# A decoder layer in fp32r pieces: four gate pairs moved ahead of attention as seven products each, branch tiles moved into attention

## The chip, the cores and the metric

The kernel runs on one core of one Trainium2 chip. Its metric is the device time of one execution in microseconds. The kernel before takes 628.67 us, the median of three runs (628.64, 628.67 and 631.46). The profiled execution took 629.03 us, of which the profile's span covers 627.3.

## The reference

The kernel computes one post-norm decoder layer on x of 512 tokens by 1024 channels, all in float32. Cut to what matters here:

```python
proj = h @ w_in                                  # 1024 -> q 512 | k 512 | v 512 | p 512 | g 2048
y_attn = moba_attention(q, k, v, rel_bias) @ w_branch_attn      # 8 heads x 64, causal, T5 bias
y_pool = multiscale_pool(p, w_pool_group, pool_scale) @ w_branch_pool
gates = sigmoid(g)                               # two gates of 1024 channels
mixed = gates[:, :, 0] * y_attn + gates[:, :, 1] * y_pool
h = layer_norm(ALPHA * h + mixed @ w_out)
a, u = split(h @ w_ffn_in)                       # 2 x 2816
f = (gelu(causal_dwconv(a)) * u) @ w_ffn_out
out = layer_norm(ALPHA * h + f)
```

With 512 tokens and blocks of 256 each token attends causally to all earlier tokens.

## The kernel before, in words

**Precision.** Every large product is made of three fp32r matmuls: each operand is split into a high part (a rounding copy, on ScalarE) and a low part (the rest, a subtraction on VectorE), and `mm3` (L247) issues hi x hi, lo x hi and hi x lo. A weight chunk of 128x1024 comes by DMA into one of three raw buffers (`wraw`, `araw`), `split` (L73) makes `whi` on ScalarE and `wlo` on VectorE, and five such slots form a ring. `weights` (L241) has up to three chunks fetched ahead of the one in use.

**Tiles.** Activations are kept transposed: channels on partitions, 512 tokens on the free axis. The tile (f) of a gate or branch is 128 output channels by 512 tokens in one PSUM bank; there are eight banks. An ordinary tile of the input projection (`in_tile`, L488) is 8 contraction steps x 3 matmuls of 512 columns.

**Seven products.** `seven` (L293) makes two tiles at once from two weight chunks by a Strassen-like scheme: weights and x are cut into 2x2 blocks, sums of blocks are formed, and seven products replace eight. One product is 4 steps x 3 matmuls of 256 columns. For each pair it needs the chunks A (1024 wide), X (1024), D (512) and Y (1024); X is loaded with one plain DMA on SP's queue and a second, accumulating one on GpSimd's (POOL) queue (`fetch_raw`, L182). Y is formed on VectorE from X and A. The sums of x (`T3`, `nT1`, `nT2`, `T4`, each as hi and lo, 512 KB apiece) are the same for all pairs.

**Stages, in the order in which TensorE meets them.** The v projection; two ordinary pooling tiles; five pairs by seven products (pool 0 and 1, then q and k in four pairs), with the pooling mixer's vector work beside them; attention for eight heads; seven branch tiles (`br`, f 0 to 6, pooling half and attention half); four gate pairs (f 4 to 7) by seven products, with sums of x formed anew from x loaded again (`quad`); the last branch tile; the output projection with LayerNorm; the FFN.

**Attention.** For head h, `head(h)` makes scaled and split q and k (L441 to L452, with a DMA for each half), `scores(h)` (L533) multiplies them, adds the bias strip and takes the row maximum (L553, VectorE), exponentials with row sums (L559, ScalarE), reciprocals (L561, VectorE) and the normalisation (L564, POOL, four instructions); `trans(h)` transposes the result (L619) and copies it to `PT` with one copy on ScalarE (L621) and two on VectorE; `pv(p)` multiplies `PT` of two heads with `vv` (L632). Each step of the loop over heads also holds one ordinary gate tile (`g0`, `g8`, `g1`, ...), whose raw logits are copied to `gates` (L498); these eight tiles are f 0 to 3 of both gates.

**Order.** The program is traced in this order and a scheduler reorders it within each engine by its own cost model, so an engine's instructions stand in one fixed sequence, and each engine works its sequence strictly in order. `tc.issue_after` holds an instruction back behind another in that sequence. Tiles with one tag share buffers in turn: three bias strips, three `pp`, three raw buffers, two `PT`; a tile that takes over memory waits for the last reader of what lay there.

## Time and profile before

| | |
|---|---|
| three runs | 628.64, 628.67, 631.46 us |
| profiled execution | 629.03 us, span 627.3 us |
| TensorE (PE) busy | 617.3 us (98%) |
| VectorE (DVE) busy | 505.0 us (81%) |
| ScalarE (ACT) busy | 354.0 us (56%) |
| GpSimd (POOL) busy | 118.5 us (19%) |
| DMA | 107.70 MB, mean 172 GB/s |

In the profile PE is the TensorE matmul, PEld its weight load, and SPq and POOLq the queues from which SyncE and GpSimd issue DMAs. A matmul's listed duration overlaps the next one's, so the pace of TensorE is read from one start to the next. The same holds, by less than 0.1 us, for VectorE and ScalarE.

### The profile page before, as it was taken

The page shows a single profiled execution, that of the slowest core. Times are in us where ns is not written, and L with a number is a line of the kernel's source. Part 1 is how long each engine was busy: PE and PEld are TensorE (multiplying, and loading weights), DVE is VectorE, ACT ScalarE, POOL GpSimd, SP SyncE. Part 2 cuts the span into 40 slices and gives each one's busy share as a digit, 9 for nine tenths or more (in the row PEclk, how much of TensorE's full clock was granted, in tenths as well). Part 3 has the DMA queues.
Part 4 walks back from the last instruction along what each step waited for, and adds up shares of the span by engine and source line. Part 5 has one row for each costly group of instructions (what it writes and reads, how often), then busy time and mean ns, then how long its engine had stood idle before and what let it go on. Part 6 is the DMA issues. An engine that isn't in the chain of part 4 may idle for free.

```text
span 627.3 us, 10417 instructions
## 1 busy us (share of the span) xinstructions
PE 617.3 (98%) x3988; PEld 553.3 (88%) x3988; DVE 505.0 (81%) x780; ACT 354.0 (56%) x536; POOL 118.5 (19%) x131
## 2 busy tenths in 40 slices
PE   9999999999999999999999999999999999999994
PEld 6899998777788998889999999999999888888884
DVE  6978787776494788399998988898988769698796
ACT  6636777655634567115576566566656346555452
POOL 0133134323142101110110101011000302123302
PEclk9999999999999999999999999999999999999998
DMA  8467647522547515704568687688734995899905
GB/s 325 152 193 191 171 120 225 134 76 84 168 116 216 139 60 177 304 32 152 151 161 200 195 200 181 178 195 203 190 100 150 331 256 117 208 212 211 261 1 134
DMA packets 40545, 107.70 MB, mean 172 GB/s; under 512 B 4384, under 2 KB 4648, under 8 KB 40240
## 3 DMA queue, kind: packets, MB, share of 16 engines
q1 hardware_dynamic: 27264, 71.90, 34.2%
q0 software_dynamic: 12656, 34.10, 27.9%
q10 hardware_dynamic: 576, 1.05, 0.5%
q8 instruction: 31, 0.51, 0.3%
q14 instruction: 18, 0.15, 0.1%
HBM read 101.77 MB, written 3.17 MB: 167 GB/s over the span
## 4 chain that ended last, share of the span: by engine, by line
PE 98%; DVE 1%; DMA 1%; ACT 0%; DVEq 0%; issue 0%
PE saf L252 5%; PE saf L249 5%; PE saf L253 5%; PE fi L249 3%; PE fi L252 3%; PE v L426 3%; PE fi L253 3%; PE sbf L252 3%; PE sbf L253 2%; PE sbf L249 2%; PE br L249 2%; PE g L249 2%; PE g L253 2%; PE g L252 2%; PE br L252 2%; PE wo L252 2%
## 5 line engine op out<-in xcount | busy, mean ns | idle before, releaser
L77 ACT ACTIVATE whi<-wraw 128x1024 fp32r<-128x1024 f32 (+1 forms) x53 | 53.9, 1024 | 44.3 <-DMA wraw<-in_w_fo 8.5
L78 DVE TENSOR_TENSOR wlo<-wraw,whi 128x1024 fp32r<-128x1024 f32 (+1 forms) x53 | 65.2, 1237 | 14.3 <-ACT whi L77 14.0
L78 DVE TENSOR_TENSOR wlo<-araw,whi 128x1024 fp32r<-128x1024 f32 x52 | 63.2, 1224 | 10.2 <-ACT whi L77 9.8
L77 ACT ACTIVATE whi<-araw 128x1024 fp32r<-128x1024 f32 x52 | 54.4, 1057 | 18.1 <-PE saf L252 5.3
L199 POOL DMA_DIRECT2D xraw<-in_w_fi x15 | 18.0, 1203 | 136.4 <-DMA xraw<-in_w_fi 45.5
L77 ACT ACTIVATE whi<-tw 128x1024 fp32r<-128x1024 f32 (+1 forms) x30 | 29.4, 983 | 24.4 <-DMA tw<-in_w_fo 11.3
L78 DVE TENSOR_TENSOR wlo<-tw,whi 128x1024 fp32r<-128x1024 f32 (+1 forms) x30 | 33.3, 1126 | 8.0 <-ACT whi L77 8.0
L252 PE MATMUL sbf<-T_lo,whi 128*128 128x256 f32 x136 | 37.9, 279 | 0.0
L252 PE MATMUL saf<-nT_lo,whi 128*128 128x256 f32 x136 | 37.8, 278 | 0.0
L249 PE MATMUL saf<-nT_hi,whi 128*128 128x256 f32 x136 | 37.8, 278 | 0.0
L252 PE MATMUL saf<-hT_lo,whi 128*128 128x256 f32 x136 | 37.8, 278 | 0.0
L249 PE MATMUL saf<-hT_hi,whi 128*128 128x256 f32 x136 | 37.8, 278 | 0.0
L253 PE MATMUL saf<-hT_hi,wlo 128*128 128x256 f32 x136 | 37.7, 278 | 0.0
L249 PE MATMUL sbf<-T_hi,whi 128*128 128x256 f32 x136 | 37.7, 277 | 0.0
L253 PE MATMUL sbf<-T_hi,wlo 128*128 128x256 f32 x136 | 37.7, 277 | 0.0
L253 PE MATMUL saf<-nT_hi,wlo 128*128 128x256 f32 x136 | 37.7, 277 | 0.0
L249 PE MATMUL fi<-hT_hi,whi 128*128 128x256 f32 (+1 forms) x112 | 36.2, 328 | 0.2 <-ACT hT_hi L77 0.2
L252 PE MATMUL fi<-hT_lo,whi 128*128 128x256 f32 (+1 forms) x112 | 36.5, 327 | 0.0
L253 PE MATMUL fi<-hT_hi,wlo 128*128 128x256 f32 (+1 forms) x112 | 36.3, 326 | 0.0
L564 POOL TENSOR_SCALAR pp<-pp,rs 128x128 f32<-128x128 f32 (+3 forms) x32 | 25.2, 801 | 36.7 <-DVE rs L561 26.6
L237 POOL DMA_DIRECT2D tw<-in_w_fo x18 | 15.6, 897 | 60.7 <-DVE wlo L78 60.7
L559 ACT ACTIVATE pp<-pp,nm 128x128 f32<-128x128 f32 (+3 forms) x32 | 17.6, 552 | 15.3 <-DVE nm L556 15.2
(346 smaller groups left out, 2172.8 us busy)
## 6 DMA issues: line engine op xcount, KB each, us to landing
tw<-in_w_fo POOLq DMA_DIRECT2D x20, 512.0 KB, 8.5
araw<-in_w_fi SPq DMA_DIRECT2D x17, 512.0 KB, 3.6
xraw<-in_w_fi SPq DMA_DIRECT2D x15, 512.0 KB, 4.7
xraw<-in_w_fi POOLq DMA_DIRECT2D x15, 512.0 KB, 6.1
wraw<-in_w_c SPq DMA_DIRECT2D x10, 512.0 KB, 3.9
wraw<-in_w_fi SPq DMA_DIRECT2D x10, 512.0 KB, 4.2
wraw<-in_w_fo SPq DMA_DIRECT2D x10, 512.0 KB, 7.4
tw<-in_w_fo SPq DMA_DIRECT2D x10, 512.0 KB, 7.8
```

Source lines behind the costliest of these rows:

```text
L77: state["hi"] = nc.scalar.activation(hi, src, AF.Copy)
L78: state["lo"] = nc.vector.tensor_tensor(lo, src, hi.bitcast(F32), op=ALU.subtract)
L199: state["acc"] = nc.gpsimd.dma_start(v, bass.AP(tensor=a.tensor, offset=a.offset, ap=[[pst, pn], [u.offset + S - a.offset, 2], [est, S]]), ...
L237: nc.gpsimd.dma_start(raw, half(then[1:], sl), accum_op=ALU.add)
L249: ins = nc.tensor.matmul(out_, wh, ah, start=start, stop=False, **kw)
L252: nc.tensor.matmul(out_, wh, al, start=False, stop=False, **kw)
L253: nc.tensor.matmul(out_, wl, ah, start=False, stop=stop, **kw)
L426: nc.tensor.matmul(bs[j], xs_[j][a], (wh, wl)[b], start=kt == 0 and n == 0, stop=False)
L559: exps[h] = nc.scalar.activation(pp[:, offs[i]:offs[i] + n], pp[:, offs[i]:offs[i] + n], AF.Exp, bias=nm[:, i:i + 1], accum_out=rs[:, i:i ...
L564: nc.gpsimd.tensor_scalar(pp[:, offs[i]:offs[i] + n], pp[:, offs[i]:offs[i] + n], rs[:, i:i + 1], 1.0, op0=ALU.mult, op1=ALU.mult)
```

## The change

Gate tiles f 0 to 3 are no longer ordinary tiles inside attention. They become four pairs by seven products, run straight after the q/k pairs, with the same sums of x, which are still in memory then. Their logits are written straight to `gates`, copied and put through the sigmoid there.

In attention the place of the gate tiles is taken by the pooling halves of branch tiles f 0 to 6 (12 matmuls of 512 columns each, against 24 of a gate tile), so z is split before the loop over heads. Heads run further ahead: scores of heads 0, 1 and 2 stand among the pairs, and inside the loop `scores(h + 3)` follows step h. After attention the attention halves follow, `br6` first. The branch weights are packed anew so that a chunk holds two halves.

To make room, v is written to DRAM (`v_d`) and read back (`vv`) when the pairs are through, and the eight sums of x are written to DRAM (`form_d`) during the pairs and read back after attention, which replaces loading x again and forming the sums a second time. The copy of the attention output to `oT` and its later split become one split from PSUM.

```diff
+    add_gates(range(GSEVEN))
+    halves = [(f, 1) for f in range(KT - 1)] + [(f, 0) for f in BR0]
...
+    aside = [(n, q) for n in ("T3", "nT2", "T4", "nT1") for q in range(2)]
+    def put_aside(count):
+        with tc.issue_after(state["plain"].ins):
+            for n, q in aside[:count]:
+                nc.sync.dma_start(form_d[n, q], flat(ti[n][q]))
+        del aside[:count]
...
+    put_aside(1)
+    head(2, nms[0], exps[0])
+    scores(1)
+    for f in range(GSEVEN):
+        n = 1 + pairs + f
+        gslot[f], gslot[8 + f] = gates[:, f, :], gates[:, GSEVEN + f, :]
+        seven(("g", f), (xT_hi, xT_lo), ti, xr[1][:, 2, n % 2 * 256:n % 2 * 256 + 256], gslot[8 + f],
+              lambda ba, u, f=f: gate_raw(f, ba))
+        if f == 0:
+            put_aside(2)
+            scores(2)
+        elif f == 1:
+            head(3, nms[1], exps[1])
+    with tc.issue_after(exps[2].ins):
+        flush()
+        for f in range(GSEVEN):
+            nc.scalar.activation(gslot[f], gslot[f], AF.Sigmoid)
+            state["gate"] = nc.scalar.activation(gslot[8 + f], gslot[8 + f], AF.Sigmoid, scale=-1.0)
...
+    vv = ap.tile([P, NT, H * DH], F32, name="vv", bufs=1)
+    nc.gpsimd.dma_start(vv, v_d)
...
-        state["o"] = nc.scalar.activation(oT[:, p, :], b, AF.Copy)
+        split(oT_hi[:, p, :], oT_lo[:, p, :], b)
...
+    for k in range(4):
+        split(zT_hi[:, k, :], zT_lo[:, k, :], zT[:, k, :])
     for h in range(H):
-        if h + 2 < H:
-            head(h + 2, nms[h], exps[h])
-        if h < H - 1:
-            in_tile(*fill.pop(0))
-        if h + 2 < H:
-            scores(h + 2)
+        if h + 4 < H:
+            head(h + 4, nms[h + 2], exps[h + 2])
         with ExitStack() as held:
             if h and h % 2 == 0:
                 pv(h // 2 - 1)
                 held.enter_context(tc.issue_after(state["pv"].ins))
             trans(h)
-        if h >= 4:
-            with tc.issue_after(nms[h].ins), tc.issue_after(exps[h].ins):
-                split(zT_hi[:, h - 4, :], zT_lo[:, h - 4, :], zT[:, h - 4, :])
-        if h == H - 1:
-            in_tile(*fill.pop(0))
+        if h:
+            br_tile(h - 1, 1)
+        if h + 3 < H:
+            with tc.issue_after(state["gate"].ins):
+                scores(h + 3)
...
-        nc.gpsimd.dma_start(quads[n], xT[k.start * P:k.stop * P, t].rearrange("(k p) t -> p k t", p=P))
+    for n in ("T3", "nT2", "T4", "nT1"):
+        for q in range(2):
+            nc.gpsimd.dma_start(flat(tg[n][q]), form_d[n, q])
...
-            t_form(forms[0], tg, *quads)
```

**VectorE at the start of attention.** Before, the first `PT` copies stand between the maxima of head 2 (`nm`, from the PSUM tile `sc2`) and those of head 3:

```order
L553 ISA pp2_1185,nm2_1186<-sc2_3_1190,strip2_937 128x512
L553 ISA nm2_1186 128x1
L622 COPY PT0_1213<-tr0_1_1215 128x512
L623 COPY PT0_1213<-tr0_2_1216 128x256
L78 TENSOR_TENSOR wlo31_1329<-wraw31_1327,whi31_1328 128x1024
```

Now, with the maxima of head 3 just done, two heads' copies and the split of z stand together:

```order
L572 ISA pp3_1722,nm3_1723<-sc3_3_1727,strip3_1116 128x512
L572 ISA nm3_1723 128x1
L79 TENSOR_TENSOR wlo45_1778<-wraw45_1776,whi45_1777 128x1024
L316 TENSOR_TENSOR sag3_1534<-xr1_99,scg3_1535 128x256
L575 TENSOR_SCALAR nm3_1723<-nm3_1723 128x4
L688 COPY PT0_1703<-tr0_1_1705 128x512
L689 COPY PT0_1703<-tr0_2_1706 128x256
L688 COPY PT1_1759<-tr1_1_1761 128x512
L689 COPY PT1_1759<-tr1_2_1762 128x256
L79 TENSOR_TENSOR zT_lo_1679<-zT_78,zT_hi_1678 128x512 x3
L572 ISA pp4_1798,nm4_1799<-sc4_01_1801,strip4_1266 128x128
```

The low parts of z, which the first branch tile multiplies, have moved from the loop's second half to a place behind four copies.

**ScalarE at the same place, now.** `whi` and `zT_hi` are high parts, `gates<-sag3` is the raw copy of the last pair's logits:

```order
L578 ACT_TABLE_LOAD
L578 ACTIVATE pp3_1722,rs3_1724<-pp3_1722,nm3_1723 128x128
L578 ACTIVATE pp3_1722,rs3_1724<-pp3_1722,nm3_1723 128x256
L578 ACTIVATE pp3_1722,rs3_1724<-pp3_1722,nm3_1723 128x384
L578 ACTIVATE pp3_1722,rs3_1724<-pp3_1722,nm3_1723 128x512
L466 ACTIVATE k1_5_1751<-rk2_817 64x512
L469 ACTIVATE q1_5_1750<-rq2_1034 64x4x128
L627 ACTIVATE gates_79<-sag3_1534 128x512
L687 ACTIVATE PT1_1759<-tr1_0_1760 128x512
L78 ACTIVATE whi46_1934<-wraw46_1933 128x1024
L645 ACT_TABLE_LOAD
L645 ACTIVATE gates_79<-gates_79 128x512
```

Right ahead of these rows stand the four `zT_hi` and the `PT0` copy. The copy of head 1 stands behind the exponentials of head 3, and two table loads have come in.

**POOL at the same place, now.** `strip6` is the bias strip of head 6, `pp3` the normalisation of head 3:

```order
L399 DMA strip6_1796<-F_d_179 128x512
L653 DMA vv_1684<-v_d_180 128x2048
L399 DMA strip7_1877<-F_d_179 128x512
L583 TENSOR_SCALAR pp3_1722<-pp3_1722,rs3_1724 128x128
```

Before, `vv` lay in memory from the start; now its load is queued behind `strip6`, which waits for the maxima of head 3.

## Rows read from the trace of the kernel before

**Rows 1.** The page: span, busy time of each engine, the chain by engine.

```profile
span 627.3 us, 10417 instructions
...
PE 617.3 (98%) x3988; PEld 553.3 (88%) x3988; DVE 505.0 (81%) x780; ACT 354.0 (56%) x536; POOL 118.5 (19%) x131
...
PE 98%; DVE 1%; DMA 1%; ACT 0%; DVEq 0%; issue 0%
```

**Rows 2.** Waits of PE: line, waited for, us in total, times, longest.

```profile
PE warm_ps L341 <- DVE warm L338: 1.2, 1, 1.2
PE fi L249 <- ACT hT_hi L77: 0.2, 1, 0.2
```

**Rows 3.** Windows: length, engines' busy us, clock, DMA share, GB/s.

```profile
66.00:72.00 6.00, 6.00 (x47) 5.39 (x46) 3.51 (x7) 3.31 (x5) 0.15 (x1) 1.00 0.94 241
98.00:163.00 65.00, 65.00 (x368) 51.65 (x366) 45.44 (x106) 36.49 (x81) 20.78 (x29) 1.00 0.38 108
...
201.00:246.00 45.00, 45.00 (x365) 43.92 (x364) 34.49 (x44) 26.86 (x41) 5.07 (x4) 1.00 0.47 133
```

**Rows 4.** Timeline of PE: start, us, instruction; 512 columns, then 256.

```profile
138.05 0.39 PE L249 MATMUL g<-xT_hi,whi 128*128 128x512 f32 x1
...
142.14 0.39 PE L249 MATMUL g<-xT_hi,whi 128*128 128x512 f32 x1
```

**Rows 5.** The same, of a late gate pair.

```profile
227.74 0.28 PE L249 MATMUL sag<-xT_hi,whi 128*128 128x256 f32 x1
...
229.94 0.28 PE L252 MATMUL sag<-gnT_lo,whi 128*128 128x256 f32 x1
```

**Rows 6.** Timeline of DVE in attention.

```profile
144.66 1.22 DVE L78 TENSOR_TENSOR wlo<-wraw,whi 128x1024 fp32r<-128x1024 f32 x1
145.80 0.68 DVE L553 CUSTOM_DVE_ANT_0 pp<-sc,strip 128x512 f32<-128x512 f32 x1
...
146.41 0.68 DVE L622 COPY PT<-tr 128x512 f32<-128x512 f32 x1
147.01 0.41 DVE L623 COPY PT<-tr 128x256 f32<-128x256 f32 x1
147.34 0.16 DVE L556 TENSOR_SCALAR nm<-nm 128x4 f32<-128x4 f32 x1
```

**Rows 7.** Timeline of ACT in attention.

```profile
130.58 0.40 ACT L559 ACTIVATE pp<-pp,nm 128x128 f32<-128x128 f32 x1 [3.33 <-DVE nm L556]
...
132.90 0.63 ACT L445 ACTIVATE k<-rk 64x512 fp32r<-64x512 f32 x1
...
134.07 0.63 ACT L77 ACTIVATE zT_hi<-zT 128x512 fp32r<-128x512 f32 x1
134.61 1.04 ACT L77 ACTIVATE whi<-wraw 128x1024 fp32r<-128x1024 f32 x1
```

**Rows 8.** Timeline of ACT: the table load ahead of the first exponential.

```profile
81.34 1.28 ACT L559 ACT_TABLE_LOAD   x1 [0.48 <-DVE nm L556]
82.64 0.40 ACT L559 ACTIVATE pp<-pp,nm 128x128 f32<-128x128 f32 x1
```

**Rows 9.** DMA issues: tiles, queue, count, KB each, median us to landing.

```profile
quad<-in_xT POOLq DMA_DIRECT2D x4, 512.0 KB, 5.9
...
quad<-in_w_c POOLq DMA_DIRECT2D x4, 512.0 KB, 8.5
...
lnb<-in_lnr POOLq DMA_DIRECT2D x2, 1024.0 KB, 11.1
```

**Rows 10.** Timeline of POOL: loads of x (quad), xs and lnb.

```profile
163.83 3.04 POOL L675 DMA_DIRECT2D quad<-in_xT  x4 [10.12 <-PE ob L632]
...
255.66 2.19 POOL L757 DMA_DIRECT2D xs<-in_x  x4 [6.67 <-DVE mx_lo L78]
...
270.66 2.79 POOL L762 TENSOR_SCALAR lnb<-lnb 128x1024 f32<-128x1024 f32 x1 [12.28 <-DMA lnb<-in_lnr]
```

**Rows 11.** DMA from 154 to 206 us: GB/s in 40 slices of 1.3 us.

```profile
GB/s 328 76 0 0 13 0 0 57 343 202 388 331 343 340 19 0 0 0 2 301 101 79 298 110 140 277 280 331 280 255 268 96 32 336 247 58 343 99 203 110
```

More of the change, by code (lines that the diff above doesn't have):

```diff
@@ L101, in layer_kernel, with add_gates @@
         add_seven(("i", 1 + p), w_c[first["q"] + p], w_c[first["k"] + p])
-    fill = [("g", 8 * g + f) for f in range(GSEVEN) for g in range(2)]
-    for n, j in fill:
-        add((n, j), w_c[first[n] + j])
-    for f in range(KT - 1):
-        add(("br", f), w_br[f])
-    for f in range(GSEVEN, KT):
-        add_seven(("g", f), w_c[first["g"] + f], w_c[first["g"] + KT + f])
-    add(("br", KT - 1), w_br[KT - 1])
+    def add_gates(fs):
+        for f in fs:
+            add_seven(("g", f), w_c[first["g"] + f], w_c[first["g"] + KT + f])
+    add_gates(range(GSEVEN))
+    halves = [(f, 1) for f in range(KT - 1)] + [(f, 0) for f in BR0]
+    for c in range(KT - 1):
+        for n, part in enumerate(halves[2 * c:2 * c + 2]):
+            at["br", part] = len(chunks), n * S
+        chunks.append(w_br[c])
+    add_gates(range(GSEVEN, KT))
+    for br in range(2):
+        at["br", (KT - 1, br)] = len(chunks), br * S
+    chunks.append(w_br[KT - 1])
     WO0 = len(chunks)
@@ L374, in layer_kernel, with flat @@
     F_d = dram.tile([H, STRIP], F32, name="F_d")
+    v_d = dram.tile([P, NT, H * DH], F32, name="v_d")
+    form_d = {(n, q): dram.tile([P, D], F32, name=f"form_{n}_{q}") for n in parts for q in range(2)}
+    aside = [(n, q) for n in ("T3", "nT2", "T4", "nT1") for q in range(2)]
+    def flat(t):
+        return t.rearrange("p a c -> p (a c)").bitcast(F32)
+    def put_aside(count):
[3 more added lines that the diff above has]
+        del aside[:count]
     def load_strip(h):
@@ L518, in layer_kernel @@
     homes["i", "D"] = lambda n: xr[1][:, n % 2, :]
+    for q in "XD":
+        homes["g", q] = lambda f, q=q: homes["i", q](1 + pairs + f) if f < GSEVEN else None
     raw_q = {}
@@ L575, in layer_kernel @@
         if n == 0:
+            with tc.issue_after(state["plain"].ins):
+                nc.sync.dma_start(v_d, v_first)
             behind_sum.close()
@@ L600, in layer_kernel, with gate_raw, br_mm, br_tile @@
             scores(0)
+    def gate_raw(f, ba):
+        nc.scalar.activation(gates[:, f, :], ba, AF.Copy)
+    put_aside(1)
+    head(2, nms[0], exps[0])
[6 more added lines that the diff above has]
+        if f == 0:
+            put_aside(2)
+            scores(2)
[6 more added lines that the diff above has]
+            state["gate"] = nc.scalar.activation(gslot[8 + f], gslot[8 + f], AF.Sigmoid, scale=-1.0)
+    assert not aside
     phase.close()
     keep = keepp.enter_context(tc.tile_pool(name="keep", bufs=1, reuse_waits="tile"))
-    gates = keep.tile([P, 2 * GSEVEN, S], F32, name="gates")
-    oT = keep.tile([P, 4, S], F32, name="oT")
-    zT_hi = keep.tile([P, 4, S], F32R, name="zT_hi")
-    zT_lo = keep.tile([P, 4, S], F32R, name="zT_lo")
+    oT_hi, zT_hi, zT_lo, oT_lo = (keep.tile([P, 4, S], F32R, name=n) for n in ("oT_hi", "zT_hi", "zT_lo", "oT_lo"))
     ap = attn.enter_context(tc.tile_pool(name="ap", bufs=2, reuse_waits="tile"))
+    vv = ap.tile([P, NT, H * DH], F32, name="vv", bufs=1)
+    nc.gpsimd.dma_start(vv, v_d)
+    unused = [zT[:, n, :] for n in range(4)]
+    branch = {}
+    def br_mm(f, br, b=None, ks=range(4), pin=False):
+        i, o = at["br", (f, br)]
+        wh, wl = (t[:, o:o + S].rearrange("p (a c) -> p a c", a=4) for t in weights(i))
+        b = b or bank(f"br{f}_{br}")
+        for k in ks:
+            src = (zT_hi[:, k, :], zT_lo[:, k, :]) if br else (oT_hi[:, k, :], oT_lo[:, k, :])
+            mm3(b, (wh[:, k, :], wl[:, k, :]), src, k == 0, k == 3, pin and k == ks[0])
+        return b
+    def br_tile(f, br):
+        b = br_mm(f, br)
+        if f < GSEVEN:
+            t = gslot[8 * br + f]
+            nc.vector.tensor_tensor(t, t, b, op=ALU.mult)
+        else:
+            t = branch[f, br] = unused.pop(0)
+            nc.scalar.activation(t, b, AF.Copy)
     toff = {0: 0, 1: S, 3: S + 3 * P, 2: 2 * S}
@@ L690, in merged @@
         mts[f] = a
-    unused = [more[:, n, :] for n in range(4)]
-    forms = list(parts)
-    for f in range(KT - 1):
-        if f < GSEVEN:
-            with tc.issue_after(state["o"].ins):
-                for g in range(2):
-                    nc.scalar.activation(gslot[8 * g + f], gslot[8 * g + f], AF.Sigmoid)
-        for br in (1, 0):
-            b = br_mm(f, br)
-            if f < GSEVEN:
-                t = gslot[8 * br + f]
-                nc.vector.tensor_tensor(t, t, b, op=ALU.mult)
-            else:
-                t = branch[f, br] = unused.pop(0)
-                nc.scalar.activation(t, b, AF.Copy)
+    for f in BR0:
+        br_tile(f, 0)
         if f < GSEVEN:
@@ L1148 @@
     fo = np.asarray(w_ffn_out)[0]
+    by_branch = [cols(np.asarray(w)[0]) for w in (w_branch_attn, w_branch_pool)]
+    order = [(f, 1) for f in range(KT - 1)] + [(f, 0) for f in BR0] + [(KT - 1, 0), (KT - 1, 1)]
+    w_br = np.stack([by_branch[br][f] for f, br in order])
+    w_br = c(w_br.reshape(KT, 2, P, S).transpose(0, 2, 1, 3)).reshape(KT, P, D)
     arrays = {
```

54 lines of the change are left out of this document (16 added, 38 removed).

## The prediction

> **What bounds the kernel now.** I read the page first. TensorE is busy 617.3 of 627.3 us, and the chain of waits that ended last is TensorE for 98% of the span [rows 1]. Busy matmuls overlap, so a wait could hide in that share; the list of waits settles it: TensorE waited 1.2 us for its first operand and 0.2 us once in mid-kernel [rows 2]. From the first matmul to the end of the FFN it is never idle, at clock 1.00 in every window shown [rows 3]. A matmul less is therefore time less, and any wait that the change opens on TensorE is time more. VectorE (45.4 of 65.0 us in attention) and ScalarE (36.5 of 65.0) have room there on average [rows 3], but averages say nothing of the first heads, so the order of the engines there is worked through below.
>
> **What TensorE loses.** From 138.05 to 142.14 us lie 18 matmuls of 512 columns, 0.227 us each [rows 4]; from 227.74 to 229.94 lie 19 of 256, 0.116 us each [rows 5]. A pair of ordinary gate tiles is 2 x 24 x 0.227 = 10.9 us; seven products are 7 x 12 x 0.116 = 9.7. That is 1.2 us a pair, 4.8 us for four. Branch tiles, transposes, scores and the products with v keep their number and width and only move. The sum starts at -4.8 us.
>
> **What the pairs add beside TensorE.** Each now needs, by the durations in [rows 6, 7], about 3.5 chunks of low parts (1.14 us each on VectorE) and of high parts (1.0 on ScalarE), two additions for Y and three for the outputs: some 6.3 us of VectorE in 9.7 us. I cost this at nothing, because four pairs of just this kind run from 201 to 246 us with VectorE busy 34.5 and ScalarE 26.9 of 45.0 us and no wait on TensorE [rows 3]; the new pairs have scores and heads beside them besides, about 12 us of VectorE over four pairs that have 13 free. If that cover is gone, a low part comes late and each pair may lose up to 1 us.
>
> **What the DMA queues add.** Per pair 0.8 MB more of weights; 1 MB of v and 4 MB of sums written in the middle of the q/k pairs; the same 5 MB read back, against 2 MB of x no longer loaded. The writes go through SP's queue between the chunk loads, 512 KB at a time, about 1.5 us each at the 340 GB/s at which the loads of x flowed [rows 11]. The DMA engines are already 0.94 busy from 66 to 72 us without a wait on TensorE [rows 3], so some chunks will land later. Chunks are loaded about 10 us ahead (8.5 us to land an accumulating one [rows 9]); I take 0, with 2 us as the upper end. VectorE also loses the eight logit copies and four formings of sums, and ScalarE four copies: nothing on TensorE's path, so nothing below zero.
>
> **Where attention starts.** Here the change makes new waits. Count from the moment when the last product that reads the sums of x ends, since z's split goes to their memory. TensorE still has two score matmuls of 512 columns (0.45), ten transposes (no wider than 0.116 each, 1.1), the last product (1.4), one matmul of the first branch tile (0.23), eight of head 4's scores (four of 256, two of 384, two of 512: 1.3) and eleven more of the branch tile (2.5); it comes to the first product with v (`ob0`) at 6.9 us.
> - ScalarE, in its order, has four high parts of z (0.54 each, from 134.07 to 134.61: 2.2), the copy of head 0 (0.54), a table load (81.34 to 82.64: 1.3 [rows 8]), four exponentials of head 3 (130.58 to 132.90: 2.3), k and q of head 5 (132.90 to 134.07: 1.2), the raw copy of the logits (0.54) and only then the copy of head 1 (0.6), which `ob0` multiplies [rows 7]. Sum 8.7: TensorE waits 1.8 us.
> - VectorE has the last maximum of head 3 (done about 1.3 after waiting for the scores), a low part (1.14), one addition and the negation (0.4), two copies for each of two heads (0.60 and 0.33, twice: 1.9) and the first low part of z (0.6) [rows 6]. That is 5.4, where the branch tile wants it at 4.4: 1.0 us, which lies inside the 1.8, since `ob0` waits for ScalarE anyway.
> - `vv` on POOL's queue stands behind `strip6`, which waits for the maxima of head 3 (1.3) and takes 0.6 to issue, so it is issued at 1.9. Behind it on POOL stand only `strip7` and the normalisation of head 3, needed 10 us later. The price of 1 MB is not shown. Lower end: 5.9, the landing of 512 KB [rows 9], gives 7.8, hidden. Upper end: 11.1, the 1 MB of `lnb`, gives 13.0, a wait of 4.3 beyond the 8.7. `lnb` stood behind 2 MB of `xs` in its queue [rows 10], while the four loads of x, 2 MB, flowed in about 8 us after the first issue [rows 10, 11], so I take 7: 8.9, 0.2 beyond.
>
> The opening costs 2.0 us, between 1.0 and 6.1.
>
> [...]
>
> **The later heads.** A head now has 2.7 us of branch tile, 1.3 of scores, 1.1 of transposes and half of a 2.3 us product, some 6.3 us, where a gate tile of 5.4 made it about 9. VectorE has per head 1.7 of maxima and 0.1 of negation, 0.9 of copies, 1.5 of k and q, half a chunk (0.6), 0.6 of gating and half a split (0.3): 5.7 us; ScalarE, with two more table loads around one late sigmoid, about as much. Between a head's scores and its transposes lie about 10 us. It closes, with little room; I take 0.4 us for hops, between 0 and 5 (1 us in each of five heads).
>
> **After attention.** The eight sums and then the accumulating load of X for pair 4 stand in POOL's queue behind the last normalisation. From the last transposes to the product that needs them lie 2.3 us of `ob3`, 7 x 2.7 of branch halves and 2.8 of products, with half a branch tile before: 25 us. Seen from the end, X needs two additions and a low part, 2.4 us, so it must land by 22.7. The sums at the rate of [rows 11] take 12 us; X's plain half can be issued only when `ob3` has freed its memory (about 7 us in) and lands some 5 later, the accumulating half 8.5 after that [rows 9]: 20.5. It fits by 2 us. I take 0.
>
> **Sum.** -4.8 + 2.0 + 0.4 = -2.4 us. The profiled execution took 629.03, its span and 1.7 us around it, which stay: 626.6. The median of the runs is 0.36 less, so the forecast for it is **626.3 us**.
>
> **Rivals.**
> - *The opening is covered* (15%): ScalarE runs ahead, `PT1`, z and `vv` all come in time. Then 4.8 less at most 1.2 remain: 623.9 to 625.1. For it: ScalarE's average of 0.56 in attention [rows 3]. Against it: the order in front of `PT1` is fixed and cannot start before the sums are read.
> - *Attention is starved at every head* (14%): the round from scores through maxima, exponentials, POOL and transposes gets longer than TensorE's shorter round, or `vv` lands as `lnb` did. 3 to 5 us more than forecast: 629 to 631, no change. For it: VectorE and ScalarE near 90% of a head; against it: the heads run one further ahead.
> - *The sums come back late* (11%): the other side. POOL's queue delivers 4 MB at the pace of `xs` and `lnb` (3 MB in the 15 us from 255.7 to 270.7 [rows 10]), 20 us, and X's accumulation starts only then: 28.5 where 22.7 was free, 6 us, and another 1 to 2 while the next pair's X trails. 633 to 634. It decides as soon as X of pair 4 lands over 23 us after the last transposes; it passes the mark of slower when it is over 5.5 us late. Against it: the 2 MB of x came at 340 GB/s.
>
> **Numbers.** The forecast's own range is 625.1 to 628.3 with 60%. 0.5%, about what a measurement of this kernel can tell from no change, is 3.1 us: faster means below 625.5, slower above 631.8. Below 625.5 lie the first rival and something over a quarter of the forecast's own 60%, 0.15 + 0.17 = 0.32. Above 631.8 lies most of the last rival, 0.09. The rest, 0.59, is no change. The range that leaves out no more than 2 in 10 is 624.3 to 631.0.
>
> **What would show it.** Right: TensorE's matmuls some 4.8 us shorter in sum; a gap of about 2 us at the first product with v, released by the ScalarE copy `PT` or by `vv`, preceded by one of about 1 us at the first branch tile released by `zT_lo`; small gaps at later transposes; none at the first late pair. Wrong: the first product with v released without a wait; gaps that repeat at every head; a wait of pair 4 on `gT3` or on X's chunk; waits on `wlo` in the new pairs, which would mean that the DMA writes or VectorE were not covered.

## The result and the profile after

The changed kernel takes **639.06 us** (median of 4 runs, 637.37 to 640.64), the kernel before 629.61 beside it (4 runs, 628.64 to 631.46): a ratio of 1.0146 [1.0101, 1.0191]. It is slower by about 9 us where 2.4 us of gain were forecast, and 8 us above the upper end of the range. The profiled execution took 637.54 us, with a span of 635.8. Medians and ratios below leave out one execution of e1 and one of e10 that took over 1.5% longer than the fastest of the same kernel; e10's profile is of that one, and of its stalls only those of the late pairs are read.

The page of the kernel after, against [rows 1]: span, busy time, chain by engine.

```profile
span 635.8 us, 10781 instructions
...
PE 617.5 (97%) x4132; PEld 557.8 (88%) x4132; DVE 510.0 (80%) x792; ACT 363.7 (57%) x556; POOL 126.6 (20%) x140
...
PE 81%; DMA 7%; issue 5%; DVE 3%; ACT 1%; POOL 1%; DVEq 0%; ACTq 0%; POOLq 0%
```

TensorE was 98% of the chain and is 81% now; DMA has 7%. The waits of PE (columns as in [rows 2]) say where the chain leaves it:

```profile
PE ob L698 <- DMA vv<-v_d: 3.0, 1, 3.0
PE sag L256 <- ACT whi L78: 1.6, 3, 1.0
PE sc L569 <- DMA kl<-kl: 1.3, 1, 1.3
...
PE sag L256 <- DVE sag L316: 1.0, 1, 1.0
PE tr L685 <- DVE nm L572: 0.4, 1, 0.4
PE sbi L256 <- ACT whi L78: 0.3, 1, 0.3
PE sag L260 <- DVE wlo L79: 0.3, 1, 0.3
```

These list 7.9 us and not all. The records of matmuls overlap (512 columns are listed with 0.39 us, 256 with 0.28, and the next starts after 0.227 and 0.115), so a short wait leaves no gap. I therefore add up, over all of TensorE's matmuls, the time from one start to the next less the usual step of the first one's width (0.227 us for 512 columns, 0.115 for 256, 0.177 for 384, 0.109 for 128, rounded here, the same in both kernels). The usual steps alone sum to 610.57 us before and 605.68 after: **-4.88 us, the -4.8 of the forecast**. What is left over is stall, by stage:

| stage | before | after | difference |
|---|---|---|---|
| start | 2.89 | 2.84 | -0.05 |
| q/k pairs (to the first gate product) | 2.37 | 4.78 | +2.41 |
| new gate pairs (to the fourth's last products) | none | 2.34 | +2.34 |
| opening of attention (to the end of the second product with v) and later heads | 0.00 | 4.95 + 1.32 | +6.27 |
| late gate pairs (to the output projection) | 0.14 | 2.32 | +2.18 |
| rest | 1.42 | 1.34 | -0.08 |
| sum | 6.82 | 19.89 | +13.07 |

13.1 lost and 4.9 won make 8.2; the spans differ by 8.5, the other 0.3 lying behind the last matmul. The windows of the kernel after show the same places (columns of [rows 3], whose 66 to 72 and 201 to 246 they answer):

```profile
66.00:72.00 6.00, 5.66 (x40) 4.72 (x39) 3.97 (x7) 5.45 (x10) 1.34 (x3) 1.00 1.06 244
72.00:78.00 6.00, 6.00 (x47) 5.48 (x46) 5.87 (x8) 4.70 (x8) 0.84 (x1) 1.00 1.04 374
102.00:108.00 6.00, 5.74 (x47) 5.54 (x48) 6.00 (x9) 4.05 (x11) 6.00 (x6) 1.00 1.06 255
138.00:144.00 6.00, 4.61 (x36) 3.95 (x35) 6.00 (x14) 5.39 (x8) 1.12 (x2) 1.00 0.64 157
144.00:150.00 6.00, 3.44 (x17) 2.57 (x15) 5.93 (x16) 5.90 (x15) 1.94 (x3) 1.00 0.86 306
201.00:246.00 45.00, 43.95 (x344) 42.01 (x343) 35.10 (x42) 25.29 (x39) 12.50 (x10) 1.00 0.54 144
```

From 66 to 78 us the DMA engines are full (1.06, 1.04). From 102 to 108 VectorE and POOL are busy without a pause, and from 138 to 150 VectorE is, while TensorE stands for 4 of 12 us. The longest DMA pieces on the chain (start, us, transfer) are an accumulating load of X, the copy of `kl` that the first scores read, another X, and v:

```profile
55.02 10.81 DMA xr<-in_w_c
...
72.86 7.50 DMA kl<-kl
...
97.92 6.53 DMA xr<-in_w_c
...
141.09 9.18 DMA vv<-v_d
```

The load of v, on POOL's timeline and among the issues of 140 to 142.5 us (KB each, us to landing):

```profile
140.52 0.58 POOL L399 DMA_DIRECT2D strip<-F_d  x1 [23.53 <-DVE nm L572]
141.09 0.55 POOL L653 DMA_DIRECT2D vv<-v_d  x1
```

```profile
vv<-v_d POOLq DMA_DIRECT2D x1, 1024.0 KB, 9.2
wraw<-in_w_br SPq DMA_DIRECT2D x1, 512.0 KB, 8.0
strip<-F_d POOLq DMA_DIRECT2D x1, 256.0 KB, 6.5
```

POOL had stood idle for 23.5 us in front of `strip6`, which waits for head 3's maxima; v, behind it, went out only then and shared the engines with the strip and a weight chunk. TensorE and VectorE there (start, us, instruction, in brackets the idle time and what ended it):

```profile
141.75 0.39 PE L256 MATMUL sag<-xT_hi,whi 128*128 128x256 f32 x1 [1.04 <-DVE sag L316]
...
147.06 0.39 PE L260 MATMUL br<-zT_hi,wlo 128*128 128x512 f32 x1
```

```profile
138.06 1.22 DVE L79 TENSOR_TENSOR wlo<-wraw,whi 128x1024 fp32r<-128x1024 f32 x1
139.20 0.41 DVE L315 TENSOR_TENSOR gates<-gates,sag 128x256 f32<-128x256 f32 x1
...
140.14 1.22 DVE L79 TENSOR_TENSOR wlo<-wraw,whi 128x1024 fp32r<-128x1024 f32 x1
141.28 0.42 DVE L316 TENSOR_TENSOR sag<-xr,scg 128x256 f32<-128x256 f32 x1
```

The addition that the last gate product needs (L316) stands behind two low parts of branch chunks, 2.4 us of VectorE for tiles that are not yet due. After the matmul that starts at 147.06 TensorE does nothing until v lands at 150.3.

### The profile page after: what moved, and what is told of

It is laid out like the page before. It is cut to its first block, busy times and chain, and to the rows that moved or that the text cites. A ratio compares the mean times of both kernels' runs of the same rounds, so it can differ in the third digit from the quotient of the medians.

```text
span 635.8 us, 10781 instructions
## 1 busy us (share of the span) xinstructions
PE 617.5 (97%) x4132; PEld 557.8 (88%) x4132; DVE 510.0 (80%) x792; ACT 363.7 (57%) x556; POOL 126.6 (20%) x140
## 4 chain that ended last, share of the span: by engine, by line
PE 81%; DMA 7%; issue 5%; DVE 3%; ACT 1%; POOL 1%; DVEq 0%; ACTq 0%; POOLq 0%
PE saf L259 5%; PE saf L256 5%; PE saf L260 5%; DMA xr<-in_w_c 4%; PE fi L256 3%; PE fi L259 3%; PE v L447 3%; PE fi L260 3%; PE sbf L259 2%; PE sbf L256 2%; PE sbf L260 2%; PE wo L259 2%; PE wo L256 2%; PE wo L260 2%; PE br L256 2%
## 5 line engine op out<-in xcount | busy, mean ns | idle before, releaser
L79 DVE TENSOR_TENSOR wlo<-araw,whi 128x1024 fp32r<-128x1024 f32 x60 | 74.3, 1250 | 8.7 <-ACT whi L78 8.3
L78 ACT ACTIVATE whi<-araw 128x1024 fp32r<-128x1024 f32 x60 | 62.5, 1057 | 20.0 <-PE saf L259 5.3
L78 ACT ACTIVATE whi<-wraw 128x1024 fp32r<-128x1024 f32 (+1 forms) x45 | 45.6, 1018 | 38.8 <-DMA wraw<-in_w_fo 10.6
L79 DVE TENSOR_TENSOR wlo<-wraw,whi 128x1024 fp32r<-128x1024 f32 (+1 forms) x45 | 53.1, 1188 | 16.7 <-ACT whi L78 16.5
L583 POOL TENSOR_SCALAR pp<-pp,rs 128x128 f32<-128x128 f32 (+3 forms) x32 | 29.4, 1050 | 17.6 <-DVE rs L580 11.1
L256 PEld LDWEIGHTS saf<-nT_hi,whi 128*128 128x128 f32 x136 | 25.5, 188 | 0.0
```

Of the source, the lines that this page charges most:

```text
L78: state["hi"] = nc.scalar.activation(hi, src, AF.Copy)
L79: state["lo"] = nc.vector.tensor_tensor(lo, src, hi.bitcast(F32), op=ALU.subtract)
L256: ins = nc.tensor.matmul(out_, wh, ah, start=start, stop=False, **kw)
L583: nc.gpsimd.tensor_scalar(pp[:, offs[i]:offs[i] + n], pp[:, offs[i]:offs[i] + n], rs[:, i:i + 1], 1.0, op0=ALU.mult, op1=ALU.mult)
```

## The experiments

All stalls are worked out as above, each from one profiled execution; two executions of the changed kernel itself (e15) agree within 0.4 us in every stage but the opening. The sum holds the start too, which no edit touches and which differed between executions all the same: 2.3 to 3.3 us in most, 5.2 in e7, 4.4 in e8, 4.8 in e9. Ratios are to the kernel before, run beside each kernel.

| kernel | us | ratio [95%] | q/k | new pairs | opening | heads | late pairs | sum |
|---|---|---|---|---|---|---|---|---|
| after | 639.06 | 1.0146 [1.0101, 1.0191] | 4.78 | 2.34 | 4.95 | 1.32 | 2.32 | 19.89 |
| e15 | 640.2 | 1.0175 [1.0159, 1.0191] | 4.45 | 2.16 | 7.79 | 1.32 | 2.57 | 22.72 |
| e1 | 638.3 | 1.0137 [1.0119, 1.0156] | 2.41 | 1.15 | 6.14 | 1.32 | 3.10 | 18.77 |
| e2 | 637.64 | 1.0122 [1.0107, 1.0137] | 4.88 | 2.76 | 4.37 | 1.31 | 2.58 | 20.84 |
| e3 | 638.0 | 1.0131 [1.0118, 1.0145] | 2.37 | 2.52 | 6.72 | 1.32 | 1.88 | 19.14 |
| e4 (of before) | 633.3 | 1.0064 [1.0051, 1.0077] | 7.64 | | | | 0.14 | 11.41 |
| e5 | 638.99 | 1.0166 [1.0130, 1.0202] | 7.29 | 1.86 | 4.35 | 1.32 | 2.39 | 22.43 |
| e6 | 636.84 | 1.0122 [1.0108, 1.0136] | 4.53 | 1.12 | 5.22 | 1.25 | 1.80 | 18.81 |
| e7 | 637.06 | 1.0113 [1.0098, 1.0129] | 2.76 | 3.17 | 3.72 | 2.57 | 1.73 | 20.79 |
| e8 | 641.42 | 1.0190 [1.0171, 1.0209] | 2.40 | 5.92 | 3.72 | 2.57 | 4.78 | 25.17 |
| e9 | 637.61 | 1.0141 [1.0123, 1.0159] | 2.39 | 2.29 | 8.17 | 1.32 | 1.96 | 22.27 |
| e10 | 637.81 | 1.0154 [1.0129, 1.0179] | | | | | 2.18 | |
| e14 | 638.41 | 1.0142 [1.0126, 1.0157] | 2.40 | 2.39 | 7.03 | 1.32 | 2.28 | 19.54 |
| e16 | 636.02 | 1.0114 [1.0095, 1.0133] | 2.56 | 2.88 | 4.36 | 1.32 | 2.47 | 17.76 |
| e11 | 634.42 | 1.0091 [1.0072, 1.0109] | 2.41 | 2.88 | 1.74 | 1.26 | 2.68 | 15.59 |
| e12 | 632.51 | 1.0077 [1.0055, 1.0099] | 2.40 | 1.92 | 1.74 | 1.22 | 2.40 | 13.46 |
| e13 | 630.9 | 1.0030 [1.0013, 1.0048] | 2.37 | 1.10 | 1.74 | 1.24 | 1.40 | 12.18 |
| e17 | 628.68 | 0.9996 [0.9980, 1.0013] | 2.37 | 1.10 | 1.72 | -0.01 | 1.14 | 11.74 |

**e1, seven of the eight writes of sums left out** (all read back from the one that stays).

```
-            for n, q in aside[:count]:
+            for n, q in [k for k in aside[:count] if k == ("T3", 0)]:
...
-            nc.gpsimd.dma_start(flat(tg[n][q]), form_d[n, q])
+            nc.gpsimd.dma_start(flat(tg[n][q]), form_d["T3", 0])
```

> Left out of the changed kernel: seven of the eight writes of sums of x to DRAM (3.5 MB); after attention all eight tiles are read back from the one that is written, so the read traffic stays and the late gate tiles are computed from the wrong sums. Theory A (the DMA engines are full from 60 to 84 and at 102 to 108 us because of these writes, so that X chunks and the copies of kl land late): the stalls of TensorE before 113 us go, 0.8 at the X chunk of the third q/k pair, 1.3 at head 0's kl, 2.2 at the high parts of the new pairs; kl lands in 2 to 3 us instead of 7.5; time 4 us below the changed kernel, about 635, ratio to before 1.008. Theory B (the stalls come from VectorE and ScalarE work that the new pairs and the earlier heads bunch together): kl lands sooner but TensorE waits for the same engines, time 638 to 639, ratio 1.014.

The wait for `kl` is gone and the q/k stall back at 2.41, level with the 2.37 of the kernel before, although `kl` still took 5.1 us. The forecast of 635 was missed, 638.3: the opening stalled 6.14 us, with a granted clock of 0.72 from 144 to 150 us. The writes cause the q/k stall. What taking them away is worth in time depends on the measurement of the changed kernel beside which it is put. Against the first four runs (1.0146 [1.0101, 1.0191]) no gain of e1, e2 or e3 can be told from noise. Against e15, the same kernel with a narrower interval (1.0175 [1.0159, 1.0191]), the three lie 0.0038 to 0.0053 lower, 2.4 to 3.3 us, with intervals apart.

**e2, the products with v read another tile** (`zT_hi` in v's place), so that none waits for v's load.

```
-                state["pv"] = nc.tensor.matmul(b[e * DH:(e + 1) * DH, kb * P:], vv[:, kb, h * DH:(h + 1) * DH],
+                state["pv"] = nc.tensor.matmul(b[e * DH:(e + 1) * DH, kb * P:], zT_hi[:, kb, h * DH:(h + 1) * DH].bitcast(F32),
```

> Left out: the products of attention take the high part of z instead of v as their stationary operand; v is still written and read back, so the traffic stays, but nothing waits for it. Theory A (the 3.0 us in front of the first product are v's landing, 9.2 us instead of the 7 that were forecast): the gap there shrinks to what the ScalarE copy of head 1's transposes leaves, 0 to 1; time 2 to 3 us below the changed kernel, about 636.5, ratio to before 1.010. Theory B (ScalarE's queue in front of that copy is as long, the 1.8 us of the forecast): the gap stays near 2 and is released by PT, time 638 or more, ratio 1.013.

The 3.0 us for v are gone, the opening falls by only 0.6: other waits of 0.5 and 0.6 us stand behind it. Against e15, where the clock fell to 0.50 behind the wait for v, it falls by 3.4. The time, 637.64, lies between the two theories.

**e3, the eight writes behind the first two branch chunks' loads** (five and three), after the q/k pairs.

```
+            if i in (at["br", (0, 1)][0], at["br", (2, 1)][0]):
+                put_aside(5 if len(aside) == 8 else 3)
...
-            put_aside(1)
```

> Nothing left out: the eight writes of the sums are only moved in SP's queue, behind the first and the second chunk of branch weights (113 to 130 us), where the DMA engines stand nearly idle in the changed kernel; the order on all other engines is the same. Theory A (full DMA engines): the stalls before 113 us go as when the writes are left out, none appears in their new place, about 635, ratio to before 1.008; v may land a little later if the branch chunks slip. Theory B (VectorE and ScalarE): no change, 638 to 639, ratio 1.014.

The same 4 MB written elsewhere leave the q/k stall at 2.37. The opening takes most of that away (6.72, the clock at 0.54 and 0.61 right after the wait for v), and the time, 638.0, misses the 635 of theory A.

**e4, the kernel before with the writes added**: v and six of the sums to DRAM, where nothing reads them; the sums one, two, two and one in successive q/k pairs.

```
+            with tc.issue_after(state["plain"].ins):
+                nc.sync.dma_start(v_d, vv)
...
+            put_aside(1)
```

> The kernel before, computing all it did, plus only the DMA traffic of the changed one in the q/k pairs: 1 MB of v and six of the eight tiles of sums (3 MB) written to DRAM from the same places of SP's queue, and never read. Theory A (full DMA engines): the kernel before gets the stalls of the changed one in that stretch without any of its new vector work, a wait on the X chunk near 66 us and on kl near 79 us, 1.5 to 2.5 us, about 631, ratio 1.003. Theory B: no wait appears, ratio 1.000.

633.3 us, 4 us above before, more than the 631 expected. Its q/k stage stalls 7.64 against 2.37. Part of the 5.3 us more is the clock: its mean over the span is 0.994 where before has 0.997, by estimate 0.003 x 632 = 1.9 us, and apart from the end the page of e4 has it below 0.9 in one slice alone, at 0.8 from 79 to 95 us, behind the slice with its one long wait. That wait is of the kind seen after:

```profile
PE sc L559 <- DMA k<-k: 1.8, 1, 1.8
```

The copies of k and kl are 128 KB from SBUF to SBUF. Issues of 55 to 90 us, before, after, and with the writes late (e3):

```profile
kl<-kl SPq DMA_DIRECT2D x3, 128.0 KB, 2.2
```

```profile
kl<-kl SPq DMA_DIRECT2D x3, 128.0 KB, 6.7
```

```profile
kl<-kl SPq DMA_DIRECT2D x3, 128.0 KB, 3.7
```

So the writes alone slow the kernel before, and their absence alone repairs the q/k stage of the kernel after. Whether `kl` waits behind the writes in SP's own queue or for engines that are full whatever the queue, no run separates: the writes go out on the queue that also issues k and kl.

**e5, v ahead of `strip6` on POOL's queue**; **e14** and **e16** add late writes, two and six, or five and three.

```
+            if h == 6:
+                held.enter_context(tc.issue_after(state["vv"].ins))
```

> Nothing left out: on POOL's queue the load of v is put ahead of the strip of head 6, which stood in front of it until the maxima of head 3 were done (140.5 us); v's memory is free about 10 us earlier. So v should be issued near 131 and land by 140. Theory D (the 3.0 us are the price of v's load alone): the gap before the first product goes and the time falls by it, 634.5 to 635.5, ratio to before 1.008. Theory V (VectorE and ScalarE bound the start of attention; with v out of the way TensorE only meets them a little later, as where the products did not wait for v): most of the gap comes back at the next transposes, 0.5 to 1.2 saved, 637, ratio 1.012.

> Nothing left out: the changed kernel with the writes of the sums late (two and six) and the load of v ahead, and no other order changed. With the DMA engines no longer full from 60 to 110 us, the worth of v's place alone is measured: if VectorE and ScalarE bound the start of attention with v out of the way, 1 to 1.5 us below the kernel with late writes alone, ratio 1.011; if v's load was a price by itself, 3 us below, ratio 1.008.

> Nothing left out: the kernel with late writes (five and three, as there) and the load of v ahead, no other order changed. In the run with two and six the second branch chunk came late behind six writes, its low part stood in VectorE's order in front of head 3's maxima, and a wait of 2.75 us opened there, which hid the worth of v's place. If that reading is right, that wait falls to 0.5 here, the wait for v stays gone, and the time is 1.5 to 3 us below the kernel with late writes alone, ratio 1.009 to 1.011. If v's place is worth nothing because other waits take its room whatever the writes, ratio 1.013.

In e5 v went out at 127.45 and its wait is gone, but the q/k pairs of this kernel stalled 7.29 (a high part of X came 1.7 us late at 66 us, a low part 2.2 at 92 us), which hides the gain: inconclusive. In e14 a branch chunk came late, I take it for the six writes' sake; its low part, at 137.46, stood in VectorE's order ahead of a head's maxima:

```profile
PE tr L685 <- DVE nm L577: 2.6, 1, 2.6
```

One wait for another. e16 is the clean one: v issued at 126.03, landed in 7.2 us, no wait for it, and against e3, which differs by this edit alone, 2.4 us less in the opening (6.72 to 4.36; about 1.6 of that is the clock, 0.54 and 0.61 from 149 to 153 us in e3 and 1.00 from 140 to 158 in e16). The ratio, 1.0131 in e3, is 1.0114, about as expected, though the two intervals overlap.

**e6, v ahead, and VectorE and ScalarE reordered at the opening** (z's split ahead of the sigmoids; branch chunks from the third on held until head 4's exponentials, then three at once); **e7** with late writes; **e8** with two steps of the new and late pairs later.

```
+    for k in range(4):
+        split(zT_hi[:, k, :], zT_lo[:, k, :], zT[:, k, :])
+    with tc.issue_after(exps[2].ins):
...
+            with tc.issue_after(nms[4].ins), tc.issue_after(exps[4].ins):
+                while state["next"] <= state["limit"]:
+                    fetch()
```

e8's own edit, against e7:

```
+         ("g", GSEVEN + 1, "X"): 2}
...
         if f == 0:
-            scores(2)
+            pass
         elif f == 1:
+            scores(2)
```

> Nothing left out: v ahead as in the run beside it, and besides that VectorE and ScalarE are relieved where attention starts: z is split before the sigmoids and the last product's close, the splits of branch chunks three to six (1.2 us each on VectorE and 1.0 on ScalarE; two of them stood at 138 and 140 us in front of the sum that the closing product reads) are held until head 4's exponentials are out, and the last two sigmoids stand together, two table loads of 1.3 us less. Theory V: the stalls from 139 to 160 us, some 6 us, fall to 2 or less and the time to 633 to 634, ratio 1.006. Theory D: no more than v ahead alone gives, within 0.5 us of that run.

> Nothing left out: the relieved start of attention and the eight writes of sums moved to the idle stretch of the DMA engines. If the 2.3 us that the moved writes saved before 100 us were lost again only because VectorE and ScalarE bound the start of attention and TensorE's clock fell behind the wait for v, the two savings now add: 631 to 632, ratio 1.003. If something else holds the time after 113 us, it equals the run with the relieved start alone.

> Nothing left out: as the run beside it, and head 2's scores one pair later (two heads' maxima and exponentials stood within 20 us of the first two new pairs, where VectorE was full from 102 to 114 us), and the chunk X of the second late pair loaded later, so that the first late pair's X need not share the DMA engines with it. Theory V: the 2.2 us of waits at 101 to 112 us and the 1.1 us at the first late pair fall to 1 us together, 629 to 630, ratio 1.000. If these waits are set by DMA alone, nothing changes against the run beside it.

The opening up to the first product with v fell to 0.77 in e6, but three high parts in a row (152.40 to 155.24 on ScalarE) then stood ahead of the next head's copies:

```profile
PE br L256 <- ACT PT L699: 1.6, 1, 1.6
...
PE tr L697 <- DVE gates L682: 0.8, 1, 0.8
```

The clock fell behind these waits too (0.57 from 156 to 160 us). So e6, at 636.84, missed its 633 to 634, and e7, at 637.06, its 631 to 632: it equals e6, as its second case had it. e8 was a miss as well: the new pairs stalled 5.92, the late ones 4.78. It made two edits at once, and which of them did this stays open.

**e9, heads 0 to 2 not normalised** (with late writes); **e10, the four sums of gated halves on VectorE** instead of POOL.

```
-        for i in range(NT):
+        for i in range(NT if h > 2 else 0):
```

```
-        nc.gpsimd.tensor_tensor(a, b, a, op=ALU.add)
+        (nc.vector if f < GSEVEN else nc.gpsimd).tensor_tensor(a, b, a, op=ALU.add)
```

> Left out: the normalisation on POOL of the softmax of heads 0 to 2; otherwise the kernel with the writes of the sums moved late. In the changed kernel these 12 POOL instructions run from 88 to 114 us beside the first new pairs, take up to 4.3 us instead of 0.4 to 0.8, and VectorE's low part beside them takes 1.92 instead of 1.22 us. Theory P (POOL and VectorE slow each other when both work on tiles in SBUF, and this makes the high and low parts of the first new pairs late): VectorE's instructions from 98 to 114 us go back to their usual length and the waits at 98 to 112 us, 1.6 us in the kernel with late writes, fall to 0.5 or less; time 1 us below that kernel, ratio 1.011. Theory O (the waits come from the order on VectorE and ScalarE alone, maxima and exponentials in front of the weights): no change, ratio 1.013.

> Nothing left out: the changed kernel with the four sums of gated halves that stand on POOL at 203.6 to 209.1 us put on VectorE instead, 0.7 us each there. Theory P: VectorE's sum for Y of pair 4, which took 2.95 us beside them, takes 0.7, and the wait of 1.1 us at the first late pair goes; ratio 1.013 against 1.0146. Theory T (the wait is the late X chunk, issued behind the sums read back from DRAM, as in the rival of the forecast): the wait stays at 1.1.

POOL's normalisation and VectorE's low parts are both longer where they run together; e9 shows that the one lengthens the other on VectorE's side. POOL (a head took 2.5 to 4.0 us before) and VectorE of the kernel after:

```profile
102.09 5.67 POOL L583 TENSOR_SCALAR pp<-pp,rs 128x128 f32<-128x128 f32 x4
```

```profile
102.63 1.92 DVE L79 TENSOR_TENSOR wlo<-araw,whi 128x1024 fp32r<-128x1024 f32 x1
```

and VectorE of e9, with two low parts in one row:

```profile
101.55 2.35 DVE L79 TENSOR_TENSOR wlo<-araw,whi 128x1024 fp32r<-128x1024 f32 x2
```

1.92 us for the first where it takes 1.22 alone [rows 6]. The stalls around 102 us fell in e9, but one of 1.7 at 125 us took their place (X of the last new pair came late; I put that down to the five writes). A stall at that place, 0.4 to 2.1 us, shows in every kernel with late writes of five and three but e3, and in none with two and six (e13, e14, e17), which speaks for it. Of e9 against e3, the time is the same, as theory O had it, though VectorE's instructions went back to their length, as theory P had it. In e10 the addition of the late pair's X took 0.69 us instead of 2.95, yet the wait that follows stayed at 1.1: POOL's sums do not cause the late stall.

**e11 to e17: the edits together.** e11 has v ahead, z's split early, the branch chunks held one at a time, late writes, and e10's edit. e12 adds head 1's and 2's normalisation held behind the last accumulating load of the new pairs:

```
+        elif f == 3:
+            with tc.issue_after(state["acc"].ins):
+                while late:
+                    late.pop(0)()
```

e13 writes two and six, issues the high parts of the first late pair's X, D and Y ahead of the copy `gy` on ScalarE, and was meant to join the last product with v, which stayed cut; e17 keeps the branch tiles behind the last product with v:

```
+            with tc.issue_after(state["hi_Y"].ins):
+                opened = seven_open(("g", f), (xT_hi, xT_lo), gy[:, own])
...
+        with tc.issue_after(state["pv"].ins):
+            br_tile(f, 0)
```

> Nothing left out: late writes, v ahead, z split early, the last two sigmoids together, the four sums on VectorE, and the branch chunks three and four split one at a time behind the exponentials of heads 5 and 7 instead of three in a row behind head 4's, which had put 3.1 us of ScalarE in front of a copy that TensorE waited for (1.7 and 1.0 us at 153 to 156 us). If the stalls are as read, one each with its own cause, what is left is the 1.6 us at 98 to 112 us and small ones: stalls of 2 us instead of 13, 628 to 631, ratio 1.000 (0.997 to 1.004). If the start of attention is bound by the sum of the work of VectorE, ScalarE and POOL there, the stalls come back at the next heads and the ratio stays at 1.010.

> Nothing left out: as the run beside it, and the normalisations of heads 1 and 2 held on POOL behind the last accumulating load of the new pairs, into the stretch from 117 to 130 us where VectorE has room. Theory P: the waits at 98 to 112 us fall by about 1 us against the run beside it. Theory O: they stay.

> Nothing left out: as the best so far (late writes, now two and six; v ahead; z early; normalisations of heads 1 and 2 held), and two orders more. The first late pair's high parts of X, D and Y stand on ScalarE ahead of the copy of y that waits for TensorE, behind which they stood although X had landed 3 us before; and the last product with v is issued in one piece behind three quarters of the first attention-branch tile, where two of its matmuls stood apart and cost 1.0 us more. Theory S (each of these waits is an order on one in-order engine): the 1.1 us at the first late pair go to 0.3, the 1.3 us at the last product with v to 0.4; about 2 us below the best so far, 630.5, ratio to before 1.003 (1.000 to 1.006). Theory T (the sums and X come back from DRAM too late whatever the order): the wait at the first late pair stays at 1.1 and the ratio at 1.007.

> Nothing left out: as the kernel with most orders changed (ratio 1.003), and the attention-branch tiles held behind the last product with v, which there was still cut in two (2 and 14 matmuls). If the cut costs the 1.2 us that the starts of the matmuls show, 1 us less, ratio 1.0015 (0.999 to 1.003). If TensorE then waits as long for the last transposes' copies, no change, 1.003.

Each took off its stage: the opening to 1.74 (e11), the new pairs to 1.92 (e12, where the waits at 102 and 108 us go) and then 1.10 (e13, where the one near 125 us goes), the late pairs to 1.40, the later heads to nothing. e11 as a whole missed its forecast of 628 to 631 by over 3 us; e13 and e17 came in theirs. What made the late stall is ScalarE's order. e12, then e13:

```profile
201.14 0.60 ACT L694 ACTIVATE gates<-br 128x512 f32<-128x512 f32 x1 [2.12 <-PE br L262]
202.59 0.39 ACT L299 ACTIVATE gy<-sag 128x256 f32<-128x256 f32 x1 [0.85 <-PE sag L262]
202.87 1.57 ACT L78 ACTIVATE whi<-quad 128x1024 fp32r<-128x1024 f32 x2
```

```profile
200.83 0.60 ACT L695 ACTIVATE gates<-br 128x512 f32<-128x512 f32 x1 [2.12 <-PE br L263]
201.33 1.57 ACT L78 ACTIVATE whi<-quad 128x1024 fp32r<-128x1024 f32 x2
```

In e12 the high parts wait behind `gy`, and `gy` 0.85 us for TensorE; in e13 they go first. And what made the later heads' stall is one product with v that the schedule cut in two, with branch work between; TensorE of the kernel after, then e17:

```profile
184.75 1.07 PE L698 MATMUL ob<-PT,vv 128*64 128x512 f32 x2
...
188.96 2.37 PE L698 MATMUL ob<-PT,vv 128*64 128x512 f32 x14
```

```profile
180.34 2.37 PE L720 MATMUL ob<-PT,vv 128*64 128x512 f32 x16
```

Two matmuls cost 1.07 us alone, sixteen 2.37. e17 ends at 628.68 us (12 runs, 627.55 to 633.13), level with the kernel before: 11.74 - 6.82 = 4.92 us more stall for 4.88 less work. It is the best version found, and it gains nothing.

**e15, the changed kernel again**, unaltered.

> The changed kernel once more, unaltered. If its stalls before 100 us come from DMA engines that are full, they differ from run to run (0.2 to 6 us at kl and at the X chunks in the profiles so far) and its times spread over 3 us or more where the kernel before spreads over 1.5; ratio to before 1.013 to 1.018. If they come from the order on the engines, the profile repeats that of the first to within 0.3 us, and the spread is that of the kernel before.

640.2 us; only the opening differs by more than 0.4 us, 7.79 against 4.95. The q/k pairs repeated their stall, 4.45 after 4.78, and the five times lie within 2.5 us, so what was expected of full DMA engines, a stall that differs from run to run, is not seen here; in e5, with the same writes, it was 7.29. Which of the two holds stays open. TensorE waits 2.98 us for v, as in the first execution (2.96), and afterwards its clock is at 0.50 of full speed; e15, then the execution first shown:

```profile
149.00:151.00 2.00, 1.18 (x4) 0.59 (x6) 1.91 (x3) 1.97 (x3) 2.00 (x2) 0.50 0.65 169
151.00:153.00 2.00, 2.00 (x8) 0.69 (x6) 0.00 (x0) 1.98 (x5) 0.97 (x2) 0.50 0.42 132
153.00:155.00 2.00, 2.00 (x14) 1.34 (x11) 0.00 (x0) 2.00 (x7) 0.00 (x0) 0.50 0.34 133
```

```profile
151.00:153.00 2.00, 2.00 (x19) 1.19 (x15) 0.60 (x1) 1.98 (x3) 1.63 (x2) 1.00 0.31 78
```

19 matmuls in those 2 us at clock 1.00, 8 at 0.50. The difference of 2.8 us is that between the two pairs of run times, 637.4 and 637.5 against 640.6 and 640.6. That the clock made those too is likely, but no trace of them shows it. The execution first shown is the exception: after a wait for v of 2.6 to 3.3 us the clock fell in e1 (0.72 from 144 to 150 us), e3 (0.54 from 149 to 151), e9 (0.83 from 140 to 160) and e15, at a cost of 1.6 to 2.9 us each, and stayed in that one alone. In e15 the late load of v thus cost about twice its wait: 2.98 us of waiting and 2.8 of clock.

## Why the prediction was wrong

- **What TensorE loses: right**, -4.88 for -4.8. The forecast's own numbers, not rounded up to 1.2 us a pair, give -4.6.
- **What the DMA queues add: failed, "I take 0, with 2 us as the upper end".** It cost 2.4 us in the q/k pairs. The step looked at chunk loads, which run 10 us ahead, and at one window where engines 0.94 busy hurt nobody [rows 3]. It left out the copies of k and kl, which have no such lead: 2.2 us became 6.7. And an accumulating load of X, 8.5 us in [rows 9], took 10.81 on the chain. e1, e3 and e4 show the writes as the cause, from both sides.
- **What the pairs add: sized too low.** 2.3 us where 0 was taken, inside the "up to 1 us" a pair. The average of four late pairs [rows 3] was the wrong witness: they had no normalisation on POOL beside their low parts. e9 shows the lengthening on VectorE, e12 that the waits go when the normalisation is held back; the rest went with the place of the late writes (e13).
- **Where attention starts: 4.95 for 2.0, in the range (1.0 to 6.1), for another reason.** Counted from the same moment (138.42 us), `vv` was issued at 2.7 instead of 1.9 and took 9.2 instead of 7, so it landed at 11.9 instead of 8.9 and released `ob0`; `PT1`, done at 10.3 instead of 8.7, lies hidden behind it. For the price of this 1 MB load the traces have 5.9 (e6), 7.2 (e16) and 9.2 with other loads beside it. The step also counted one low part on VectorE where two branch chunks' stood in front of L316: 1.04 us. And it had no price for a clock that falls behind a wait (2.8 us in e15).
- **The later heads: 0.4 forecast, 1.3 measured, inside 0 to 5.** The head's round did close. The loss was `ob3` cut in two, a cost of order that no average shows (e17).
- **After attention: failed, "It fits by 2 us. I take 0".** X landed at 206.7 us, 23.5 after the last transposes where 22.7 was allowed, but nothing waited for it or for the sums; 2.2 us went all the same, over half of it since ScalarE's high parts stood behind `gy` (e13). The step counted VectorE's work in front of the product and not the place in ScalarE's queue.
- **The rivals.** That TensorE waits for sums that come back late did not happen. The starved attention came true in part, `vv` late, without gaps at every head. The time was above every rival, because each of them let one thing go wrong, and here four stages each lost 2 to 6 us. e1, e2, e3 and e5 each took a wait away and moved the ratio by 0.0024 or less against the first runs and by 0.0009 to 0.0053 against e15's. Some of what they saved was lost to waits that stood behind (e2), some to the clock (e1, e3), and e5's is hidden by other stalls; v ahead, late writes and the reorderings of e11 to e17 together moved the ratio by 0.015, over 9 us.

## What to carry to other kernels

Where one engine is never idle, a change that shortens its work pays only if every other queue keeps its lead (here 4.9 us were won and 13.1 lost): list what is copied or loaded with the shortest lead (here SBUF copies of 128 KB, 2.2 us before and 6.7 after, and one load behind a waiting one), and price added traffic by that, not by the chunk loads. Put DRAM writes where nothing with a short lead is in flight (e3: the q/k stall from 4.78 to 2.37), and issue a load as soon as its memory is free, ahead of anything on its queue that waits (e16 against e3: the opening from 6.72 to 4.36). When several waits are opened at once, taking one away can show the next, and a wait can cost the clock behind it besides (2.8 us in e15), so account by stage, and run the changed kernel itself more than once, before judging an edit by its time.

## What the runs showed of the hardware that was not expected

- A 128 KB copy within SBUF took 2.2 us where the DMA engines were 0.58 busy (55 to 90 us, before) and 6.7 where they were 0.98 (after, same stretch); between these, 3.7 at 0.83 (e3) and 5.1 at 0.87 (e1).
- A low part on VectorE took 1.92 us beside POOL's normalisation, where it took 1.22 alone and two took 2.35 without that normalisation (e9). An addition took 2.95 beside POOL's sums and 0.69 with those sums moved to VectorE (e10). POOL's normalisation of one head took 5.67 us beside the low parts, 2.5 to 4.0 in the kernel before. Whether VectorE was blocked or slowed in its 0.70 us more the record doesn't tell.
- After TensorE had stood for 3.0 us the granted clock stayed at 1.00 in one execution and fell to 0.50 for six microseconds in another of the same kernel (e15), at a cost of 2.8 us. It fell in e1, e3 and e9 as well, after 2.6, 3.1 and 3.3 us, to 0.72 from 144 to 150, 0.54 from 149 to 151 and 0.83 from 140 to 160 us.
